# A seven-product MLP: the up stage makes two block sums of its activations and none of w_down, the down stage makes the others

## The chip, the core and the metric

The kernel runs on one core of a Trainium2 chip. The metric is the device time of one execution in microseconds. The core has five engines with queues of their own: TensorE (PE, with PEld for its weight loads), VectorE (DVE), ScalarE (ACT), GpSimd (POOL) and SyncE (SP, which here only issues transfers). ACT and POOL issue transfers too. A transfer of one block is 128x512 float32, 256 KB.

## The reference, cut to what matters

One decoder layer on 2048 tokens of width 1024: a token mixer, then an MLP with 4096 hidden units. Only the MLP is touched by the change:

```python
x = x + _rmsnorm(mix, norm_mix_post[i])
h = _rmsnorm(x, norm_mlp_pre[i])
f = jnp.square(jax.nn.relu(jnp.einsum("btd,df->btf", h, w_up[i])))
f = jnp.einsum("btf,fd->btd", f, w_down[i])
x = x + _rmsnorm(f, norm_mlp_post[i])
```

## The kernel before, in words

**Precision.** Every float32 operand of a large matmul is split into a high and a low part (`split`, L493 to L497: ACT copies the high part, L495, and DVE subtracts it, L496), and a product is three matmuls, high by high, high by low, low by high.

**Seven products for eight.** Both MLP matmuls are done on 2x2 blocks with the Strassen-Winograd scheme, which needs seven block products, numbered 0 to 6 and always walked in `ORDER` 0, 1, 5, 6, 4, 2, 3. The left operand of product 0 to 3 is a11, a12, s4, a22, of product 4, 5, 6 it is s1, s2, s3, where s1 = a21+a22, s2 = s1-a11, s3 = a11-a21, s4 = a12-s2 (`left`, L500). The right operands are b11, b21, b22, t4, t1, t2, t3 with t1 = b12-b11, t2 = b22-t1, t3 = b22-b12, t4 = b21-t2 (`right_sums`, L517).

**Mixer.** The mixer fills the first half of the time. It leaves the normed hidden states in DRAM (`h2_d`). `hidden_sums(g, k)` (L525) loads four blocks of them, scales them on ACT, makes t1 to t4 and stores seven blocks in `hs_d`. For g = 0 POOL makes these sums, for g = 1 DVE does. The pieces of work left over from the last mixer block stand in a list `pend` and are taken one by one inside the up stage by `drain(1)`, the four `hidden_sums(1, k)` as the last of them (steps 10 to 13 of g = 0).

**Up stage.** There are two token halves g, and for each of them 16 steps p, which are 32 steps. `hidden_blocks(g)` (L537) loads and splits the 28 right operands of a half, and they stay in SBUF for its 16 steps. A step is 7 products of 4 x 3 matmuls, 84 matmuls of 128x512. For it `up_weights` (L674) makes the four sums s1 to s4 of the next piece of w_up on DVE (L506, L507, L509, L512) into tiles of the tag `us`, which has 4 buffers, and splits seven operands (7 times L495 on ACT, 7 times L496 on DVE) into `wh` and `wl`, with 9 buffers each: little more than one step's. Seven additions (L708, DVE) take the products out of PSUM. ACT applies relu and square (L712, L713) and POOL makes the four sums of the activations (`summed`, L721: operands 4, 5, 6, 2 of the down stage). ACT stores the three plain blocks and POOL its four sums, so that all seven left operands of the down stage stand in DRAM (`f_d`).

**w_down in the up stage.** In 16 of the 32 steps (the table `due`, L842) four blocks of w_down are also loaded (`down_sums_load`, L677) and, behind the step, their t1 to t4 are made on DVE (`down_sums`, L686, by L519 to L522). These go to the same four `us` buffers, and from there by SP to DRAM (`dn_d`, L690).

**Down stage.** For each product in `ORDER` all 16 pieces p are accumulated in eight PSUM banks, one for each of eight sites (g, t). A step p is 8 sites x 3 matmuls, 24 matmuls (L822 to L824). `down_operands` (L748) loads one block of w (from w_down or `dn_d`) and one of f for each g, three transfers a step, and splits them. The f operands go round rings of eight steps (`ROUND`), w has 9 buffers, raw tiles of w have 6 (`raw`), raw tiles of f have 6 (`xt`). When a product is complete, `close` (L788) adds its eight banks to the accumulators. Products 2 and 3 end output rows: `half` squares and scales a half row (tile `us` for the squares), and `finish` (L769) loads the residual x1 in two tiles of the tag `uc` (10 buffers, L775), applies L776 on DVE and stores the result, one half by SP and one by ACT (L777). For the last product, 3, the last six steps are kept back and done site by site (`LATE`).

**What sets the order.** The program is written in the order above, and a scheduler (the tile framework) sorts each engine's queue by times that it estimates. The queue is then fixed, and each engine works through it in order and waits where an operand or a buffer is not there.

Of the kernel before, what the change touches and what calls it, by code (L numbers as in the profile page):

```python
# [44 lines left out]
def hybrid_layer(ctx: ExitStack, tc: tile.TileContext, x, xT, w_in, w_dt, w_out, w_up, w_down,  # L45
# [631 lines left out]
    def down_sums_load(p):  # L677
        raw = {}
        for j in range(2):
            for k in range(2):  # L680
                raw[j, k] = big("yl")
                SY.dma_start(raw[j, k].rearrange("p (a b) -> p a b", a=1),
                             w_down[2 * p + j][:, k:k + 1, :])
        return raw

    def down_sums(p, raw):  # L686
        blocks = right_sums(raw[0, 0], raw[0, 1], raw[1, 0], raw[1, 1], V)
        for i in ORDER:
            if i > 2:
                SY.dma_start(dn_d[p][i], blocks[i])  # L690

    turn = [0]

    def up(g, p, hb7, wb7):
# [24 lines left out]
        def summed(i, a, b, op):  # L719
            c = big("fs")  # L720
            G.tensor_tensor(c, a, b, op=op)  # L721
            save(i, c, G)
            return c

# [11 lines left out]
        t1 = summed(4, a21, a22, ALU.add)
        t2 = summed(5, t1, a11, ALU.subtract)
        summed(6, a11, a21, ALU.subtract)
        a12 = relu2(plus(u3, product(3)))
        save(1, a12, S)  # L740
        summed(2, a12, t2, ALU.subtract)
# [3 lines left out]
    ROUND = (HOMES[0], HOMES[2]), (HOMES[1], HOMES[3])  # L745
    step = [0]

    def down_operands(i, p):  # L748
# [8 lines left out]
        w = split(raw, ("wh", "wl"))
        f = []
        for g in range(NG):
            raw = big("xt")  # L760
            SY.dma_start(raw, f_d[g][p][i])
# [138 lines left out]
```

## Time and profile before

| | |
|---|---|
| runs shown | median 2867.87 us (2864.69 to 2868.1), 3 runs |
| the profiled execution | 2866.95 us |
| its span | 2865.2 us, 37725 instructions |
| mixer | to 1480 us |
| up stage | first matmul at 1480.3 us, last at 2226.9 us |
| down stage | 2226.8 us to 2855.0 us, then 10.2 us with no matmul |
| busy | PE 96%, PEld 78%, DVE 66%, ACT 47%, POOL 23% |
| moved by DMA | 456.81 MB, mean 159 GB/s |

In a row of the windows the columns are: the stretch in us, its length, then for PE, PEld, DVE, ACT and POOL the busy time and the count of instructions, then the granted clock of TensorE, the busy share of the 16 DMA engines, and GB/s. Matmuls overlap in the records, so that PE's busy time has to be read together with the count. In a row of the waits stand the waiting engine, tile and line, what it waited for, the sum in us, the number of times and the longest. In a row of the timeline stand start, duration, engine, line, operation, out<-in, count, and in square brackets the idle time before it and what ended it. In a group row the two numbers behind the bar are the busy time in us and the mean ns of one.

### The profile page before, as it was taken

The numbers are of one execution on the slowest core, as the hardware profiler recorded it, in microseconds if no ns is written. First come the engines' busy times: TensorE is split into PE (matmuls) and PEld (weight loads), VectorE is DVE, ScalarE is ACT, GpSimd is POOL, SyncE is SP. The second block draws the span as 40 slices with busy tenths as digits, with TensorE's granted clock in tenths as the row PEclk, the third lists the DMA queues.
The fourth block names the chain that finished last, engine by engine and source line by source line (L and its number), as shares of the span: only waits on it lengthen the run. The fifth ranks groups of instructions, "written<-read, shape, count | busy, mean of one in ns | idle before, by whom it ended". The sixth has DMA issues, their size and how long they took to land. (4 is left out here: it accounts for less than half of the span.)

```text
span 2865.2 us, 37725 instructions
## 1 busy us (share of the span) xinstructions
PE 2747.2 (96%) x12822; PEld 2247.6 (78%) x12822; DVE 1879.9 (66%) x3351; ACT 1351.6 (47%) x2361; POOL 646.8 (23%) x578
## 2 busy tenths in 40 slices
PE   8999999999999999999999989889989999999998
PEld 6888888888888887888877767767777788888877
DVE  6674867758676677766686666796677635434564
ACT  6545545564454645555554545454445533223331
POOL 1121412114121134211122433333333101000020
PEclk9999999999999999999999999999999999999999
DMA  7323344333343327443254658775654844444364
GB/s 276 131 85 121 100 129 143 119 107 107 119 144 125 108 93 255 150 147 113 97 167 147 225 175 279 262 241 200 210 192 153 292 140 135 144 139 140 122 199 146
DMA packets 254448, 456.81 MB, mean 159 GB/s; under 512 B 28080, under 2 KB 44848, under 8 KB 254256
## 3 DMA queue, kind: packets, MB, share of 16 engines
q1 hardware_dynamic: 198032, 359.50, 38.9%
q10 hardware_dynamic: 45984, 61.36, 6.1%
q0 software_dynamic: 10240, 33.56, 3.0%
q8 instruction: 100, 1.64, 0.2%
q14 instruction: 92, 0.75, 0.1%
HBM read 338.84 MB, written 115.47 MB: 159 GB/s over the span
## 5 line engine op out<-in xcount | busy, mean ns | idle before, releaser
L154 PE MATMUL mm<-hh,wh 128*128 128x512 f32 x1408 | 555.5, 395 | 5.4 <-DVE mix L444 3.2
L155 PE MATMUL mm<-hl,wh 128*128 128x512 f32 x1408 | 551.2, 391 | 0.8 <-DVE hl L144 0.8
L156 PE MATMUL mm<-hh,wl 128*128 128x512 f32 x1408 | 550.7, 391 | 0.0
L99 DVE TENSOR_TENSOR wl<-raw,wh 128x512 fp32r<-128x512 f32 x480 | 369.0, 779 | 236.7 <-ACT wh L98 228.0
L98 ACT CAST wh<-raw 128x512 fp32r<-128x512 f32 x480 | 293.0, 617 | 461.3 <-PE mm L155 292.8
L154 PEld LDWEIGHTS mm<-hh,wh 128*128 128x128 f32 x1408 | 265.8, 189 | 60.6 <-issue 4.5
L155 PEld LDWEIGHTS mm<-hl,wh 128*128 128x128 f32 x1408 | 265.8, 189 | 56.0 <-DVE hl L144 2.2
L156 PEld LDWEIGHTS mm<-hh,wl 128*128 128x128 f32 x1408 | 265.6, 189 | 55.7
L167 PE MATMUL ax<-wl,yh 128*128 128x512 f32 x512 | 200.5, 392 | 2.2 <-DVE wl L99 2.2
L166 PE MATMUL ax<-wh,yh 128*128 128x512 f32 x512 | 200.7, 393 | 0.0
L168 PE MATMUL ax<-wh,yl 128*128 128x512 f32 x512 | 200.4, 391 | 0.0
L496 DVE TENSOR_TENSOR wl<-raw,wh 128x512 fp32r<-128x512 f32 x163 | 118.9, 733 | 106.2 <-ACT wh L495 57.7
L822 PE MATMUL ax<-wh,hl 128*128 128x512 f32 x448 | 176.0, 394 | 8.1 <-DVE acc L785 6.5
L721 POOL TENSOR_TENSOR fs<-uc 128x512 f32<-128x512 f32 x64 | 87.0, 1359 | 416.7 <-ACT uc L713 250.4
L823 PE MATMUL ax<-wl,hl 128*128 128x512 f32 x448 | 175.7, 392 | 0.0
L496 DVE TENSOR_TENSOR wl<-us,wh 128x512 fp32r<-128x512 f32 x128 | 116.2, 916 | 84.9 <-POOL fs L721 38.8
L495 ACT CAST wh<-raw 128x512 fp32r<-128x512 f32 x163 | 100.2, 618 | 146.0 <-PE ax L824 68.2
L495 ACT CAST hl<-xt 128x512 fp32r<-128x512 f32 x120 | 74.3, 620 | 145.1 <-PE ax L823 102.9
L495 ACT CAST wh<-us 128x512 fp32r<-128x512 f32 x128 | 76.7, 617 | 129.0 <-POOL fs L721 36.8
L110 POOL TENSOR_TENSOR cst<-cst 128x1 f32<-128x1 f32 (+1 forms) x76 | 61.3, 807 | 337.4 <-DVE cst L109 332.9
L767 POOL TENSOR_TENSOR acc<-acc,gain 128x512 f32<-128x512 f32 x16 | 24.5, 1553 | 500.2 <-PE ax L824 338.4
L822 PE MATMUL mm<-wh,hh 128*128 128x512 f32 x336 | 131.3, 391 | 1.1 <-DVE uc L708 1.1
(455 smaller groups left out, 6171.3 us busy)
## 6 DMA issues: line engine op xcount, KB each, us to landing
raw<-w_in_dram SPq DMA_DIRECT2D x352, 256.0 KB, 2.8
xt<-f SPq DMA_DIRECT2D x224, 256.0 KB, 2.7
raw<-w_out_dram SPq DMA_DIRECT2D x128, 256.0 KB, 2.8
f<-fs POOLq DMA_DIRECT2D x128, 256.0 KB, 3.4
f<-uc ACTq DMA_DIRECT2D x96, 256.0 KB, 2.9
raw<-w_up_dram SPq DMA_DIRECT2D x68, 256.0 KB, 3.4
row<-cs SPq DMA_DIRECT2D x64, 256.0 KB, 4.0
yl<-w_down_dram SPq DMA_DIRECT2D x64, 256.0 KB, 4.4
```

The costliest lines, as they stand in the source:

```text
L98: S.copy(hi, raw)
L99: V.tensor_sub(lo, raw, hi.bitcast(F32))
L154: PE.matmul(pt, lhsT=wh[:, ks], rhs=ah[k], start=(k == 0), stop=False)
L155: PE.matmul(pt, lhsT=wh[:, ks], rhs=al[k], start=False, stop=False)
L156: PE.matmul(pt, lhsT=wl[:, ks], rhs=ah[k], start=False, stop=(k == KT - 1))
L166: PE.matmul(pts[t], lhsT=a, rhs=wh, start=(i == 0), stop=False)
L167: PE.matmul(pts[t], lhsT=a, rhs=wl, start=False, stop=False)
L168: PE.matmul(pts[t], lhsT=c, rhs=wh, start=False, stop=(i == n - 1))
L495: S.copy(hi, v)
L496: V.tensor_sub(lo, v, hi.bitcast(F32))
L822: PE.matmul(banks[k], lhsT=fh[:, ts], rhs=wh, start=(p == 0), stop=False)
L823: PE.matmul(banks[k], lhsT=fh[:, ts], rhs=wl, start=False, stop=False)
```

## The change

The up stage now stores six blocks a step: a11, a22, a21, a12 by ACT and s1, s2 by POOL (`summed` is gone, two POOL sums are left). `down_sums_load`, `down_sums`, `due` and `dn_d` are gone. In the down stage `down_operands` loads what an operand needs and makes the difference itself: `F_PARTS` names the blocks of f (two for products 2 and 6, subtracted on POOL into `fs`), `W_PARTS` those of w (two for products 4 and 6, and for product 3 with t2 as the second; three for product 5), subtracted on DVE into `us`. Product 5 stores its t2 by ACT for product 3. A step of products 0, 1, 5, 6, 4, 2, 3 then has 3, 3, 5 (and one store), 6, 4, 5, 4 loads, where each had 3.

The buffers move with it: `half` squares into `fs` instead of `us`; `finish` takes x1 into `us` (4 buffers) instead of `uc` (10); the rings of the low parts of f have seven places, no longer eight. `hidden_sums` is made by POOL for both halves.

```diff
-        blocks = right_sums(raw[0, 0], raw[0, 1], raw[1, 0], raw[1, 1], V if g else G)
+        blocks = right_sums(raw[0, 0], raw[0, 1], raw[1, 0], raw[1, 1], G)
...
-    ROUND = (HOMES[0], HOMES[2]), (HOMES[1], HOMES[3])
+    ROUND = (HOMES[0], HOMES[2][:7]), (HOMES[1], HOMES[3][:7])
...
+    F_PARTS = (("a11",), ("a12",), ("a12", "s2"), ("a22",), ("s1",), ("s2",), ("a11", "a21"))
+    W_PARTS = ((0, 0),), ((1, 0),), ((1, 1),), ((1, 0), None), ((0, 1), (0, 0)), \
+        ((0, 1), (0, 0), (1, 1)), ((1, 1), (0, 1))
...
+        ws = []
+        for at in W_PARTS[i]:
+            raw = big("raw")
+            if at is None:
+                SY.dma_start(raw, t2_d[p])
+            else:
+                j, k = at
+                SY.dma_start(raw.rearrange("p (a b) -> p a b", a=1),
+                             w_down[2 * p + j][:, k:k + 1, :])
+            ws.append(raw)
+        v = ws[0] if len(ws) == 1 else less(V, "us", ws[0], ws[1])
+        if len(ws) == 3:
+            v = less(V, "us", ws[2], v)
+            S.dma_start(t2_d[p], v)
+        w = split(v, ("wh", "wl"))
         f = []
         for g in range(NG):
-            raw = big("xt")
-            SY.dma_start(raw, f_d[g][p][i])
-            f.append(split(raw, [r[n % len(r)] for r in ROUND[g]]))
+            fs = []
+            for part in F_PARTS[i]:
+                fs.append(big("xt"))
+                SY.dma_start(fs[-1], f_d[g][p][part])
+            v = fs[0] if len(fs) == 1 else less(G, "fs", *fs)
+            f.append(split(v, [r[n % len(r)] for r in ROUND[g]]))
...
     def half(m, s2, tok, i, eng):
-        S.activation(big("us"), m, AF.Square, accum_out=s2[:, i:i + 1])
+        S.activation(big("fs"), m, AF.Square, accum_out=s2[:, i:i + 1])
...
         for i in range(2):
-            xt = big("uc")
+            xt = big("us")
             SY.dma_start(xt, x1_d[tok][:, i * 512:(i + 1) * 512])
...
-            if due[g][p]:
-                dn = ahead.pop(0)
-                draw = down_sums_load(dn)
             up(g, p, hb7, wb7)
             drain(1)
-            if due[g][p]:
-                down_sums(dn, draw)
```

**DVE in the second half of the up stage.** Before, the four sums of w_down (L519 to L522, reading `yl`) stand between the sums of w_up (L506 to L512), the splits (L496) and the additions out of PSUM (L708):

```order
L512 TENSOR_TENSOR us<-raw,us 128x512
L519 TENSOR_TENSOR us<-yl 128x512
L496 TENSOR_TENSOR wl<-us,wh 128x512 x2
L520 TENSOR_TENSOR us<-yl,us 128x512
L496 TENSOR_TENSOR wl<-raw,wh 128x512
L521 TENSOR_TENSOR us<-yl 128x512
L708 TENSOR_TENSOR uc<-uc,ax 128x512
L708 TENSOR_TENSOR uc<-uc,mm 128x512
L522 TENSOR_TENSOR us<-yl,us 128x512
L496 TENSOR_TENSOR wl<-yh,wh 128x512 x2
```

Now, at the same kind of place (the addition is L693 there):

```order
L512 TENSOR_TENSOR us<-raw,us 128x512
L496 TENSOR_TENSOR wl<-us,wh 128x512
L693 TENSOR_TENSOR uc<-uc,mm 128x512
L496 TENSOR_TENSOR wl<-us,wh 128x512
L693 TENSOR_TENSOR uc<-uc,ax 128x512
L506 TENSOR_TENSOR us<-yh 128x512
L693 TENSOR_TENSOR uc<-uc,mm 128x512
```

The four L519 to L522 rows are gone, and with them the other users of the four `us` buffers in this half.

**DVE at the passage from product 2 to product 3 in the down stage.** Before, the last splits ahead of product 2's first closing addition (L785) belong to product 3, those of its weights (`wl<-raw`) among them:

```order
L496 TENSOR_TENSOR wl<-raw,wh 128x512
L496 TENSOR_TENSOR m<-xt,hh 128x512
L496 TENSOR_TENSOR scm<-xt,hl 128x512
L496 TENSOR_TENSOR wl<-raw,wh 128x512
L496 TENSOR_TENSOR m<-xt,hh 128x512
L496 TENSOR_TENSOR xd<-xt,hl 128x512
L496 TENSOR_TENSOR wl<-raw,wh 128x512
L496 TENSOR_TENSOR m<-xt,hh 128x512
L496 TENSOR_TENSOR xdh<-xt,hl 128x512
L785 TENSOR_TENSOR acc<-acc,mm 128x512 x3
```

Now only splits of product 3's f blocks stand there. Its first weight difference (L734, `us<-raw`) and weight split (`wl<-us`) come behind all but one of the 16 L776 of `finish`, these rows being the end of them:

```order
L776 SCALAR_TENSOR_TENSOR us<-acc,cst,us 128x512
L109 TENSOR_SCALAR cst<-cst 128x1
L776 SCALAR_TENSOR_TENSOR us<-acc,cst,us 128x512 x5
L734 TENSOR_TENSOR us<-raw 128x512
L776 SCALAR_TENSOR_TENSOR us<-acc,cst,us 128x512
L496 TENSOR_TENSOR wl<-us,wh 128x512
L734 TENSOR_TENSOR us<-raw 128x512 x2
L496 TENSOR_TENSOR wl<-us,wh 128x512 x2
```

So the weights of product 3 moved from ahead of the closing of product 2 to behind its `finish`, since x1 and these differences share the four `us` buffers.

**SP at the same passage.** Now the loads of x1 (L775, `us<-x`) alternate with the stores of finished rows (L777), each load waiting for a `us` buffer:

```order
L777 DMA out_dram<-us 128x512
L775 DMA us<-x_2_79 128x512
L777 DMA out_dram<-us 128x512
L775 DMA us<-x_2_79 128x512
L775 DMA us<-x_3_80 128x512
L777 DMA out_dram<-us 128x512
L775 DMA us<-x_3_80 128x512
L775 DMA us<-x_8_85 128x512
```

Before, the ten tiles of tokens 0 to 3 and 8 were loaded ahead of the first of these stores; now the four of tokens 0 and 1.

More of the change, by code (lines that the diff above doesn't have):

```diff
@@ L475, in hybrid_layer @@
     ORDER = (0, 1, 5, 6, 4, 2, 3)
-    f_d = [[[dram.tile([P, TB], F32, name=f"f{g}_{p}_{i}") for i in B7]
+    f_d = [[{i: dram.tile([P, TB], F32, name=f"f{g}_{p}_{i}")
+             for i in ("a11", "a12", "a21", "a22", "s1", "s2")}
             for p in range(NP)] for g in range(NG)]
-    dn_d = [[dram.tile([P, 512], F32, name=f"dn{p}_{i}") if i > 2 else None for i in B7]
-            for p in range(NP)]
+    t2_d = [dram.tile([P, 512], F32, name=f"t2_{p}") for p in range(NP)]
     hs_d = [[[dram.tile([P, TB], F32, name=f"hs{g}_{i}_{k}") for k in range(4)]
@@ L675, in up_weights @@
         return left(raw[0, 0], raw[0, 1], raw[1, 0], raw[1, 1], V)
[L677 to L690, printed above, removed]
     turn = [0]
@@ L717, in save @@
             q.dma_start(f_d[g][p][i], c)
[L719 to L723, printed above, removed]
         s1 = big("uc")
@@ L727, in up @@
         a11 = relu2(plus(s1, product(1)))
-        save(0, a11, S)
+        save("a11", a11, S)
         u2 = plus(s1, product(5))
@@ L733, in up, with less @@
         a22 = relu2(plus(u3, p5))
-        save(3, a22, S)
+        save("a22", a22, S)
         a21 = relu2(plus(u4, product(2)))
[L736 to L741, printed above, removed]
+        save("a21", a21, S)
+        t1, t2 = big("fs"), big("fs")
+        G.tensor_tensor(t1, a21, a22, op=ALU.add)
+        save("s1", t1, G)
+        G.tensor_tensor(t2, t1, a11, op=ALU.subtract)
+        save("s2", t2, G)
+        save("a12", relu2(plus(u3, product(3))), S)
     LATE = 6
-    ROUND = (HOMES[0], HOMES[2]), (HOMES[1], HOMES[3])
+    ROUND = (HOMES[0], HOMES[2][:7]), (HOMES[1], HOMES[3][:7])
     step = [0]
+    F_PARTS = (("a11",), ("a12",), ("a12", "s2"), ("a22",), ("s1",), ("s2",), ("a11", "a21"))
+    W_PARTS = ((0, 0),), ((1, 0),), ((1, 1),), ((1, 0), None), ((0, 1), (0, 0)), \
+        ((0, 1), (0, 0), (1, 1)), ((1, 1), (0, 1))
+    def less(eng, tag, a, b):
+        c = big(tag)
+        eng.tensor_tensor(c, a, b, op=ALU.subtract)
+        return c
     def down_operands(i, p):
@@ L839, in down_stage @@
                 close(i, k, banks[k])
-    ahead = list(range(NP))
-    due = [[p in at for p in range(NP)] for at in
-           ((3, 5, 7, 9, 11, 13, 15), (3, 4, 6, 7, 8, 10, 11, 12, 14))]
     raw = up_load(0, 0)
```

7 lines of the change are left out of this document (removed).

## The prediction

> **What bounds the kernel now.** I read the page first, then the windows cut at the steps of the up stage, then PE's waits, then the timelines at two places. PE is busy for 96% of the span, so the question is where it is not, or at which clock.
>
> ```profile
> PE 2747.2 (96%) x12822; PEld 2247.6 (78%) x12822; DVE 1879.9 (66%) x3351; ACT 1351.6 (47%) x2361; POOL 646.8 (23%) x578
> ...
> 1480.27:1554.10 73.83, 66.18 (x273) 53.30 (x272) 46.37 (x65) 31.69 (x54) 17.47 (x18) 0.93 0.51 168
> 1554.10:1853.30 299.20, 266.55 (x1125) 212.85 (x1125) 205.25 (x299) 146.99 (x263) 107.34 (x111) 0.96 0.69 233
> 1853.30:1927.90 74.60, 61.18 (x253) 48.52 (x252) 71.89 (x94) 45.22 (x82) 24.98 (x24) 0.91 0.70 240
> 1927.90:2226.90 299.00, 278.72 (x1178) 223.87 (x1177) 210.44 (x285) 133.28 (x227) 106.91 (x112) 0.97 0.56 192
> 1927.90:1946.97 19.07, 19.07 (x86) 15.79 (x85) 13.41 (x17) 8.59 (x15) 7.78 (x8) 1.00 0.50 167
> 2007.50:2035.10 27.60, 22.96 (x85) 17.15 (x84) 17.09 (x27) 9.81 (x17) 7.68 (x8) 0.88 0.53 184
> 2330.00:2762.00 432.00, 432.00 (x1907) 357.48 (x1906) 190.58 (x285) 142.93 (x266) 15.50 (x12) 1.00 0.45 139
> ```
>
> The last row is PE undisturbed: 432.00 / 1907 = 0.2265 us a matmul, 5.44 us a down step of 24, 19.0 us an up step of 84. The row of 1927.90 is such an up step; that of 2007.50, the same work, took 27.6 us, at a granted clock of 0.88. Lost time of a stretch is its length less 0.2265 us a matmul: steps 0 and 1 of the first half 73.8 - 61.8 = 12.0; its steps 2 to 14 299.2 - 254.8 = 44.4; step 15 and steps 0 and 1 of the second half 74.6 - 57.3 = 17.3; the rest 299.0 - 266.8 = 32.2. That is 105.9 us in the up stage, while 2330 to 2762 of the down stage loses nothing. What PE waits for in the up stage:
>
> ```profile
> PE mm L703 <- DVE wl L496: 32.4, 14, 5.0
> PE mm L701 <- ACT wh L495: 18.7, 9, 6.0
> PE ax L703 <- DVE wl L496: 10.3, 9, 2.1
> ```
>
> So it waits for the split weights. DVE is not busy all the time there, but it is held up. Two rows of POOL and one of DVE show by what:
>
> ```profile
> 2017.63 1.30 POOL L721 TENSOR_TENSOR fs<-fs,uc 128x512 f32<-128x512 f32 x1
> 2018.88 1.28 POOL L721 TENSOR_TENSOR fs<-uc 128x512 f32<-128x512 f32 x1
> ...
> 2020.20 0.69 DVE L512 TENSOR_TENSOR us<-raw,us 128x512 f32<-128x512 f32 x1 [2.72 <-POOL fs L721]
> ...
> 2028.98 0.69 DVE L521 TENSOR_TENSOR us<-yl 128x512 f32<-128x512 f32 x1 [1.81 <-DMA f<-fs]
> ```
>
> DVE's L512, with two SBUF inputs, begins 0.04 us after POOL's second sum ends (2020.16). Such DVE operations and POOL's sums take turns. The last row is a stall inside a sum of w_down.
>
> ```profile
> 2009.88 0.69 DVE L708 TENSOR_TENSOR uc<-uc,mm 128x512 f32<-128x512 f32 x1 [1.98 <-DMA f<-fs]
> ...
> L721 POOL TENSOR_TENSOR fs<-uc 128x512 f32<-128x512 f32 x64 | 87.0, 1359 | 416.7 <-ACT uc L713 250.4
> L496 DVE TENSOR_TENSOR wl<-us,wh 128x512 fp32r<-128x512 f32 x128 | 116.2, 916 | 84.9 <-POOL fs L721 38.8
> ...
> L496 DVE TENSOR_TENSOR wl<-raw,wh 128x512 fp32r<-128x512 f32 x109 | 78.1, 717 | 89.1 <-ACT wh L495 50.0 <-PE ax L823 32.7 <-DMA uc<-x 5.3
> ...
> L495 ACT CAST wh<-us 128x512 fp32r<-128x512 f32 x128 | 76.7, 617 | 129.0 <-POOL fs L721 36.8
> ...
> L776 DVE SCALAR_TENSOR_TENSOR uc<-acc,cst,uc 128x512 f32<-128x512 f32 x32 | 25.7, 844 | 8.1 <-POOL cst L110 8.1
> ```
>
> The split itself agrees: 916 ns in the up stage (first L496 row), 717 in the down stage (second), where POOL is nearly idle.
>
> **The up stage, part by part.** I price a step as if DVE's operations with two SBUF inputs and POOL's sums never overlap. Before: 11 of the former (4 sums, 7 splits) at 0.69 = 7.6, 4 POOL sums at 1.36 = 5.4, 7 additions out of PSUM at 0.69 = 4.8, together 17.8 us, under PE's 19.0. A step that also makes sums of w_down has 4 x 0.69 = 2.8 more: 20.6, over it, with the stores' waits on top. After: 7.6 + 2.7 + 4.8 = 15.1 us, so that 3.9 us a step are spare. The Trainium skill, "SBUF — State Buffer", section "Who interferes with whom", has this as a lock on one port pair: a two-input VectorE instruction and a GpSimd one that reads SBUF block each other for the whole instruction. The three rows agree; by it the sum stays as it is below, and were the two engines independent, the steps that I charge for POOL's work would lose nothing and the gain of 70 would be 80.
>
> What stays lost: steps 0 and 1, which begin with `hidden_blocks`, 12.0. The passage between the halves splits 28 blocks, 28 x 0.69 = 19.3 us of DVE in one step; it had four sums of w_down as well (2.8, and a stall like the 1.81), so 17.3 falls to about 13. Steps 10 to 13 make `hidden_sums` on POOL now, four more sums of 1.36: 15.1 + 5.4 = 20.5, 1.5 us over PE's 19.0 in each, 6 us; made by DVE they would need 15.1 + 2.8 = 17.9 and lose nothing. The four steps that end rows of the mixer carry two POOL and two DVE operations more, by the nearest rows 2 x 1.36 + 2 x 0.84 = 4.4: 19.5, with their small operations 1 us over in each, 4 us. Together 12.0 + 13 + 10 + 1 = 36, where 105.9 were lost: **gain 70 us**. From below: only the DVE time of the 64 sums, 64 x 0.69 = 44. From above: all but steps 0 and 1, 94. I take the working between them, because steps without sums in the second half already run at 19.07. Removed transfers (64 loads, 64 stores on SP, 32 stores of f) cost nothing by themselves; ACT's extra store of a21 lies in 8.6 to 9.8 us of busy ACT out of 19.
>
> **The down stage, products 5, 6, 4, 2.** They gain loads, DVE and POOL work, and operands are far ahead: SP waits there for PE, that is, for a ring place to come free.
>
> ```profile
> SPq L761 <- PE ax L824: 257.0, 117, 12.0
> 2226.00:2244.00 18.00, 12.75 (x39) 8.73 (x38) 18.00 (x27) 14.06 (x27) 6.34 (x6) 0.72 0.97 340
> ```
>
> Products 5 and 6 move six blocks a step, 1.573 MB in 5.44 us, 289 GB/s; the window above moved 340 through the same buffers. Product 6 on the turn-taking pair: one difference and three splits 4 x 0.69 = 2.8, two POOL differences 2.7, 5.5 us against 5.44. Seven ring places are 38 us of lead, which absorbs that and a passing shortage. I take **0**, up to 15 lost if the lead runs out.
>
> **The passage from product 2 to product 3.** This is the cost. Before:
>
> ```profile
> 2758.52 0.39 PE L824 MATMUL ax<-wh,xdl 128*128 128x512 f32 x1
> 2758.74 0.39 PE L822 MATMUL mm<-wh,hh 128*128 128x512 f32 x1
> ...
> 2766.00 0.39 PE L824 MATMUL mm<-wh,row 128*128 128x512 f32 x1
> 2772.91 0.79 PE L822 MATMUL ax<-wh,hl 128*128 128x512 f32 x1 [6.52 <-DVE acc L785]
> ...
> 2777.69 0.40 PE L824 MATMUL mm<-wh,row 128*128 128x512 f32 x1
> ...
> 2754.73 1.88 DVE L785 TENSOR_TENSOR acc<-acc,mm 128x512 f32<-128x512 f32 x3
> ...
> 2767.13 2.41 DVE L776 SCALAR_TENSOR_TENSOR uc<-acc,cst,uc 128x512 f32<-128x512 f32 x2 [0.45 <-POOL cst L110]
> ...
> 2760.70 3.48 DVE L776 SCALAR_TENSOR_TENSOR uc<-acc,cst,uc 128x512 f32<-128x512 f32 x2 [0.46 <-POOL cst L110]
> 2768.91 1.00 ACTq L777 DMA_DIRECT2D out_dram<-uc  x2
> ...
> 2787.99 1.41 DVE L776 SCALAR_TENSOR_TENSOR uc<-acc,cst,uc 128x512 f32<-128x512 f32 x2 [0.44 <-POOL cst L110]
> ...
> xt<-f SPq DMA_DIRECT2D x224, 256.0 KB, 2.7
> ...
> uc<-x SPq DMA_DIRECT2D x32, 256.0 KB, 5.2
> out_dram<-uc SPq DMA_DIRECT2D x16, 256.0 KB, 2.1
> out_dram<-uc ACTq DMA_DIRECT2D x16, 256.0 KB, 3.8
> ```
>
> PE went on with product 3 at 2758.74, stopped at 2766.00 for a bank and restarted at 2772.91, the next 11 matmuls taking 4.8 us where 2.5 are due: 6.7 us of hole and 2 of clock, 8.7. After, PE needs product 3's first weights, and these stand on DVE behind the L776 of `finish`. If x1 is always there, the 16 L776 end at 2789.4 as before; with difference 0.69, copy 0.62 and split 0.69 PE starts at 2791.4. But x1 has four buffers. The first two tokens' L776 end by 2769.5, and three more rounds follow of L776 0.84, store 3.0 (the mean of 2.1 and 3.8) and load, 3.5 (an estimate: the 2.7 of a load of f and 0.8 of SP's queue) to 5.2: 7.3 to 9.0 us each. The last round ends at 2791.5 to 2796.6; I take 2794 and a restart at 2796. PE has been idle since 2758.7: 37.3 and 2 for the clock, 39.3, less the 8.7 of before: **loss 31 us**. From below 2791.4, 26; from above rounds of 12 us (before, ACT issued the first stores only at 2768.91, 4.7 us behind the end of the L776 that began at 2760.70), 2805.5 and 2807.5, 42.
>
> Behind that, a step of product 3 needs 0.69 + 3 x 0.69 = 2.8 us of DVE in 5.44 and has its f splits ready: nothing more. In the tail the eight `finish` share the four buffers again. A site closes every 4.4 us (below, the first two after the first), so a tile has 8.8 us from one token to the next but one, against a store and a load of 3.0 + 3.5 to 5.2 and L776: about 1 us lost, 0 to 6.
>
> ```profile
> 2826.44 0.69 DVE L785 TENSOR_TENSOR acc<-acc,mm 128x512 f32<-128x512 f32 x1 [19.05 <-PE mm L824]
> 2830.86 0.68 DVE L785 TENSOR_TENSOR acc<-acc,mm 128x512 f32<-128x512 f32 x1
> ...
> 2226.90:2240.00 13.10, 7.85 (x21) 4.79 (x20) 13.10 (x21) 11.66 (x22) 3.13 (x3) 0.67 0.94 320
> ```
>
> The start of the down stage (last row: 13.1 us with 21 matmuls, so 8.3 lost) has the same splits in the same order: 0, plus or minus 4.
>
> **The sum.** -70 + 0 + 31 + 1 = -38 us. Against the profiled execution, 2866.95 us (span 2865.2 and 1.75 around it), that is 2829; the median of the runs shown, 2867.87, is 0.9 higher: **2830 us**.
>
> **Rivals.**
> A. My forecast: 0.64. Its own range: a gain of 80 with a loss of 26, to a gain of 58 with a loss of 40 and 5 beside it: 2814 to 2855.
> B. The passage costs nothing more, since SP and ACT get x1 through in time and PE's hole stays near that of before: -70 + 1, 2799 us. For it: only four L776 wait for a load if landings take under 3 us. Against: the order itself puts product 3's weights behind `finish`, whatever the loads do. 0.05.
> C. The up stage stays short of DVE or ACT: steps with leftovers from the mixer and `hidden_sums` on POOL still lose, so only the 44 us come back, and the passage costs its 42: 2867 and no change, or 2856 with 31. For it: the four `us` buffers are still shared with `hidden_sums`, whose stores ACT issues in order behind POOL. 0.19, a quarter of it near no change.
> D. Slower: the transfers of products 5 and 6 don't keep up. At 192 GB/s, the rate of the second half of the up stage, six blocks take 8.2 us a step, 2.75 over PE's, 88 us in 32 steps; less 38 of lead, 50 lost; product 2 with five blocks 6.8 us, 22 more: -70 + 31 + 1 + 72 = +34, 2902 us. It decides from a loss of 38, that is 76 us of shortage in those 32 steps, 7.8 us a step or 202 GB/s. For it: four xt tiles a step go through six buffers, so that a tile may take 8.2 us from issue to issue, of which 5.2 can be the landing and 1.4 POOL. Against: 340 GB/s in the window above. 0.07.
> Half of what is left over, 0.05, I give to each side.
> The Trainium skill, "DMA: Bandwidth & Descriptors", section "Specifications", gives about 358 GB/s for a core's share of HBM, by which 289 fits and D would not come; no trace here shows a limit of that kind.
>
> About 0.2% (5.7 us) is what a measurement of this kernel can tell from no change. Faster by more: 0.86; within: 0.05; slower: 0.09. The range of 2805 to 2860 takes in A, most of C's milder half, and leaves out B's end and D.
>
> **What would show it.** Right: the windows of the up stage's second half at 19.0 to 19.2 us a step with granted clock 1.00; PE's waits for L496 and L495 there mostly gone; a single PE hole of 30 to 45 us between products 2 and 3, ended by DVE's split of `wl<-us`; products 5 and 6 with no idle PE. Wrong: holes in products 5 or 6 with DMA near its full share (D); up steps still at 20 us and more with DVE waiting for POOL or for `us` (C); a hole of under 20 us at the passage (B).

## The result, and the profile after

The changed kernel takes 2790.06 us, median of 4 runs (2788.24 to 2791.79), beside 2867.98 us for the kernel before on the same chip (2864.69 to 2868.7): ratio 0.973, 95% interval 0.9714 to 0.9747. The gain is 78 us where 38 were forecast, and the time lies 15 us under the range. The profiled span is 2787.5 us, 77.7 less. The page's first part, and the groups that stand for L496 with `us` and for one of POOL's two sums a step:

```profile
PE 2711.5 (97%) x12822; PEld 2235.0 (80%) x12822; DVE 1883.7 (68%) x3351; ACT 1351.6 (48%) x2361; POOL 639.9 (23%) x530
...
L496 DVE TENSOR_TENSOR wl<-us,wh 128x512 fp32r<-128x512 f32 x192 | 148.8, 778 | 114.6 <-ACT wh L495 65.8 <-PE ax L823 14.9 <-PE ax L824 6.9
...
L717 POOL TENSOR_TENSOR fs<-uc 128x512 f32<-128x512 f32 x32 | 42.6, 1332 | 398.2 <-ACT uc L698 208.6 <-DVE wl L496 85.7 <-PE mm L688 46.3
```

DVE, ACT and POOL are as busy as before. What changed is when. The windows at the same stages, then products 5 and 6, then the passage from product 2 to product 3:

```profile
1478.50:1546.50 68.00, 62.64 (x273) 51.07 (x272) 44.85 (x68) 31.01 (x54) 10.95 (x10) 0.97 0.54 179
1546.50:1801.50 255.00, 253.40 (x1125) 209.18 (x1125) 181.93 (x262) 146.87 (x268) 84.73 (x79) 0.99 0.61 206
1801.50:1863.00 61.50, 58.93 (x253) 46.84 (x253) 56.83 (x84) 41.75 (x76) 11.72 (x12) 1.00 0.70 238
1863.00:2129.70 266.70, 266.70 (x1178) 220.83 (x1177) 184.71 (x265) 143.28 (x244) 52.31 (x56) 1.00 0.42 146
2129.70:2142.90 13.20, 13.20 (x60) 10.94 (x59) 9.68 (x14) 6.80 (x13) 3.96 (x4) 1.00 1.01 356
2303.70:2390.70 87.00, 87.00 (x385) 72.04 (x384) 64.48 (x79) 30.30 (x56) 37.73 (x25) 1.00 0.85 293
2390.70:2477.70 87.00, 87.00 (x385) 72.06 (x384) 54.14 (x73) 27.34 (x48) 20.16 (x13) 1.00 0.68 226
2651.90:2686.10 34.20, 0.15 (x2) 0.07 (x1) 25.78 (x43) 8.03 (x23) 17.04 (x15) 0.57 0.67 213
```

By the prediction's measure (length less 0.2265 us a matmul) the up stage now loses 6.2, 0.2, 4.2 and -0.1 us in the four stretches, 10.5 where it lost 105.9: 95.4 us came from there. The start of the down stage, 13.2 us with 60 matmuls, loses nothing (9.6 before over the whole product 0). Products 5 and 6 have no idle PE. The passage costs a hole of 34 us. Together -95.4 - 9.5 + 27.7 (the passage, 37.0 lost where 9.3 were) + 1.3 (the tail) - 1.8 (the mixer) = -77.7 us. PE's waits from 1470 us on:

```profile
PE mm L822 <- ACT wh L495: 34.0, 1, 34.0
PE mm L686 <- ACT wh L495: 4.9, 1, 4.9
PE mm L687 <- DVE xdt L496: 1.9, 1, 1.9
PE ax L688 <- DVE wl L496: 1.4, 1, 1.4
```

The 61 us of waits for split weights in the up stage (the three rows shown for the kernel before) are down to 6. The one long wait is the passage; in its timeline stand PE's last matmul of product 2 and its first of product 3, and what DVE did between:

```profile
2651.60 0.39 PE L824 MATMUL ax<-wh,scm 128*128 128x512 f32 x1
2686.03 1.22 PE L822 MATMUL mm<-wh,hh 128*128 128x512 f32 x2 [34.05 <-ACT wh L495]
...
2647.27 2.05 DVE L785 TENSOR_TENSOR acc<-acc,mm 128x512 f32<-128x512 f32 x3 [10.87 <-PE mm L824]
...
2681.84 1.41 DVE L776 SCALAR_TENSOR_TENSOR us<-acc,cst,us 128x512 f32<-128x512 f32 x2 [3.43 <-DMA us<-x]
2683.98 0.75 DVE L776 SCALAR_TENSOR_TENSOR us<-acc,cst,us 128x512 f32<-128x512 f32 x1 [0.73 <-DMA us<-x]
2684.65 0.68 DVE L734 TENSOR_TENSOR us<-raw 128x512 f32<-128x512 f32 x1
```

Product 3's difference (L734) stands behind all but one of the L776, as forecast; the restart came 38.8 us behind the first L785, where 41.3 were forecast.

### The profile page after: what moved, and what is told of

Its sections match the earlier page's. It is cut to its first block, busy times and chain, and to the rows that moved or that the text cites. A ratio compares the mean times of both kernels' runs of the same rounds, so it can differ in the third digit from the quotient of the medians.

```text
span 2787.5 us, 37716 instructions
## 1 busy us (share of the span) xinstructions
PE 2711.5 (97%) x12822; PEld 2235.0 (80%) x12822; DVE 1883.7 (68%) x3351; ACT 1351.6 (48%) x2361; POOL 639.9 (23%) x530
## 4 chain that ended last, share of the span: by engine, by line
PE 90%; DVE 4%; DMA 3%; issue 1%; POOL 1%; ACT 1%; ACTq 0%; SPq 0%; DVEq 0%; POOLq 0%
PE mm L155 11%; PE mm L154 11%; PE mm L156 11%; PE ax L824 4%; PE ax L822 4%; PE ax L823 4%; PE ax L166 4%; PE ax L168 4%; PE ax L167 4%; PE ax L688 3%; PE ax L686 3%; PE ax L687 3%; PE mm L687 3%; PE mm L688 3%; PE mm L686 3%; PE mm L823 3%
## 5 line engine op out<-in xcount | busy, mean ns | idle before, releaser
L99 DVE TENSOR_TENSOR wl<-raw,wh 128x512 fp32r<-128x512 f32 x480 | 368.5, 778 | 241.7 <-ACT wh L98 230.5
L98 ACT CAST wh<-raw 128x512 fp32r<-128x512 f32 x480 | 293.0, 617 | 464.1 <-PE mm L155 294.3
L496 DVE TENSOR_TENSOR wl<-us,wh 128x512 fp32r<-128x512 f32 x192 | 148.8, 778 | 114.6 <-ACT wh L495 65.8
L495 ACT CAST wh<-us 128x512 fp32r<-128x512 f32 x192 | 114.7, 616 | 95.5 <-DVE us L509 26.6
L496 DVE TENSOR_TENSOR wl<-raw,wh 128x512 fp32r<-128x512 f32 x99 | 79.1, 803 | 107.9 <-ACT wh L495 56.8
L734 POOL TENSOR_TENSOR fs<-xt 128x512 f32<-128x512 f32 x64 | 94.9, 1490 | 197.9 <-DMA xt<-f_s 99.4
L717 POOL TENSOR_TENSOR fs<-uc 128x512 f32<-128x512 f32 x32 | 42.6, 1332 | 398.2 <-ACT uc L698 208.6
L823 PE MATMUL mm<-wl,hh 128*128 128x512 f32 x336 | 131.6, 392 | 0.3 <-DVE wl L496 0.3
L697 ACT ACTIVATE uc<-uc 128x512 f32<-128x512 f32 x128 | 80.7, 631 | 101.2 <-DVE uc L693 89.6
```

What stands on the lines that cost most here:

```text
L98: S.copy(hi, raw)
L99: V.tensor_sub(lo, raw, hi.bitcast(F32))
L496: V.tensor_sub(lo, v, hi.bitcast(F32))
L823: PE.matmul(banks[k], lhsT=fh[:, ts], rhs=wl, start=False, stop=False)
```

## The experiments

Three theories of the unexpected gain in the up stage are tried: **turns** (DVE's operations with two SBUF inputs and POOL's sums exclude each other, the prediction's price), **held buffers** (the four `us` buffers wait for SP's stores), **transfers** (the loads and stores of the w_down sums were not free). For the passage, **order** (product 3's split behind `finish`) stands against **four buffers** for x1.

The table gives all runs. "Lost" is length less 0.2265 us a matmul between the first matmuls of the steps, from the profiled run; steps 2 to 14 hold small mixer matmuls that are shorter, so that -3.4 there is nothing lost. (The windows above also count matmuls that reach across an edge, hence 6.2 there and 6.4 here.) The ratio is to the kernel before as measured beside that run; its median there was 2862.58 to 2867.98 us, so that the times alone don't tell apart runs that differ by less than 5 us. "Lead" is how long before PE's first matmul with an operand DVE had ended its split, the mean of the seven operands of the step.

| run | time us (ratio to before, 95%) | lost: steps 0-1 | 2-14 | 15-17 | 18-31 | product 0 | products 2, 3 | lead at step 24, 31 |
|---|---|---|---|---|---|---|---|---|
| before | 2867.98 | 12.3 | 44.6 | 17.5 | 32.5 | 9.6 | 9.3 | 1.0, 7.5 |
| after | 2790.06 (0.9714-0.9747) | 6.4 | 0.4 | 4.4 | 0.2 | 0.1 | 37.0 | 16.0, 20.1 |
| e1 | 2770.18 (0.9669-0.9698) | 7.1 | -3.4 | 5.7 | 0.2 | 0.1 | 20.4 | 16.0, 20.1 |
| e2 | 2850.22 (0.9947-0.9976) | 9.6 | 61.0 | 16.7 | 2.8 | 12.1 | 9.1 | 7.6, 3.3 |
| e3 | 2801.01 (0.9779-0.9808) | 10.3 | 28.9 | 11.9 | 0.2 | 1.9 | 8.3 | 7.7, 12.8 |
| e4 | 2784.87 (0.9723-0.9754) | 8.5 | 14.9 | 10.3 | 0.2 | 5.5 | 10.0 | 16.8, 12.0 |
| e5 | 2785.22 (0.9698-0.9733) | 8.5 | -3.4 | 1.9 | 0.2 | 0.1 | 37.8 | 16.0, 20.1 |
| e6 | 2807.18 (0.9766-0.9809) | 11.9 | 5.6 | 9.6 | 0.2 | 0.1 | 38.0 | 14.7, 18.3 |
| e7 | 2873.65 (1.0016-1.0037) | 10.0 | 39.1 | 13.4 | 19.3 | 8.3 | 37.5 | 1.8, 5.8 |
| e8 | 2780.89 (0.9682-0.9718) | 9.8 | -1.1 | 6.4 | 0.2 | 0.1 | 27.5 | 16.0, 20.1 |
| e9 | 2767.7 (0.9641-0.967) | 8.2 | -3.4 | 3.2 | 0.2 | 0.1 | 19.7 | 16.0, 20.1 |
| e10 | 2758.95 (0.961-0.9639) | 8.1 | -3.4 | 4.6 | 0.2 | 0.1 | 8.3 | 16.0, 20.1 |
| e11 | 2761.29 (0.9619-0.9652) | 7.2 | -1.7 | 6.4 | 0.2 | 0.1 | 6.0 | 16.0, 20.1 |
| e12 | 2801.11 (0.9753-0.9782) | 8.6 | 36.2 | 4.9 | 0.2 | 0.1 | 8.8 | 10.8, 18.7 |
| e13 | 2827.48 (0.9852-0.9885) | 7.1 | 38.6 | 2.6 | 0.2 | 0.1 | 36.9 | 15.8, 20.1 |
| e14 | 2800.14 (0.9755-0.9786) | 7.8 | -0.8 | 14.5 | 0.2 | 0.1 | 38.6 | 15.2, 19.4 |
| e15 | 2752.51 (0.9593-0.9621) | 8.5 | -3.4 | 3.8 | 0.2 | 0.1 | 6.1 | 16.0, 20.1 |
| e16 | 2830.77 (0.9865-0.9894) | 12.6 | 31.5 | 10.8 | 0.2 | 0.1 | 36.2 | 16.2, 18.4 |
| e17 | 2812.0 (0.9799-0.9829) | 10.8 | 30.9 | 7.1 | 12.2 | 1.2 | 9.1 | 1.2, 13.4 |
| e18 | 2864.13 (0.9984-1.0005) | 14.1 | 58.8 | 12.2 | 21.1 | 10.5 | 9.1 | 1.3, 4.0 |

### The two parts alone: e3 and e4

e3 is the kernel before with the activation part (two POOL sums, the rest in the down stage; rings of seven, squares in `fs`):

> The kernel before with the activation part of the change alone: two sums on POOL in the up stage, differences of f on POOL in the down stage (with the rings of seven and the squares of half in fs, without which it does not fit into SBUF); the sums of w_down stay in the up stage, in the us buffers. T1: a step with sums needs 7.6 + 2.8 + 2.7 + 4.8 = 17.9 us, under PE's 19.0, so some 60 us come back: 2800 to 2815 us. T2: the us buffers are held as before, at most 25 us come back: 2843 to 2868 us.

e4 is the changed kernel with the four activation sums back on POOL, `hidden_sums` of g = 1 on DVE and x1 in `uc`:

> The w_down part of the change alone: no sums of w_down in the up stage, differences of w on DVE in the down stage; the four activation sums stay on POOL in the up stage, hidden_sums of the second half stays on DVE, and x1 stays in the uc buffers. T1: 17.8 us a step, under 19.0, the ordinary steps lose nothing but those with hidden_sums (20.6) and mixer leftovers (over 21) lose 15 or so: 2805 to 2820 us. T2: all the ordinary steps are free, those with hidden_sums lose some us as their sums sit in the us buffers: 2785 to 2800 us. If POOL's four sums are what lengthens steps 0 and 1, the passage between the halves and the start of the down stage, these lose 12, 13 and 8 us as before; if not, they are shorter by themselves.

Either part alone takes away the whole loss of steps 18 to 31, so that loss needed both. By the table, up stage and product 0 together lost 116.5 us before; e3 takes away 63 of it, e4 77, the whole change 105. The two parts are 140 together, 35 too many, and 32 of these are what both regain in steps 18 to 31. Elsewhere the gains nearly add: in steps 2 to 14 they are 15.7 and 29.7, and the whole change gains 44.2. The hole of the passage is in neither part (8.3 and 10.0 us lost in products 2 and 3).

### What the turns cost: e7, e6, e14

More POOL sums in each up step, four in e7 and, with `range(2)`, two in e6:

```diff
         save("s2", t2, G)
+        for _ in range(4):
+            G.tensor_tensor(big("fs"), a21, a22, op=ALU.add)
```

> The same with four more unread POOL sums a step, six in all. Turn-taking in full: 7.6 + 6 x 1.36 + 4.8 = 20.6 us a step against PE's 19.04; 1.5 us in each of 14 undisturbed steps of the second half, 21 us, 1.5 us in those of the first, 20, and the disturbed steps as with two more sums: 2835 to 2855 us, with up steps of 20.5 us in a row. If POOL's work displaces DVE only where an operation with two SBUF inputs happens to meet a sum (DVE's additions out of PSUM can lie beside them): second half 19.04, 2795 to 2812 us.

Windows of e7 over steps 18 to 23, 25 to 29, 30 and 31, then POOL and DVE in step 26:

```profile
1914.30:2028.50 114.20, 114.20 (x505) 94.57 (x504) 78.75 (x103) 52.39 (x93) 51.03 (x45) 1.00 0.39 134
2048.70:2151.50 102.80, 98.02 (x421) 78.03 (x420) 74.11 (x94) 45.24 (x81) 46.01 (x39) 1.00 0.34 121
...
2151.50:2176.50 25.00, 22.03 (x85) 17.70 (x84) 11.97 (x19) 10.68 (x18) 13.05 (x12) 0.86 0.28 103
2176.50:2199.90 23.40, 19.23 (x85) 15.61 (x84) 15.21 (x21) 15.67 (x29) 11.40 (x11) 0.99 0.45 147
```

```profile
2069.03 6.07 POOL L722 TENSOR_TENSOR fs<-uc 128x512 f32<-128x512 f32 x4
...
2068.76 2.13 DVE L496 TENSOR_TENSOR wl<-raw,wh 128x512 fp32r<-128x512 f32 x1 [3.67 <-DMA f_s<-fs]
2070.82 1.77 DVE L507 TENSOR_TENSOR us<-us,raw 128x512 f32<-128x512 f32 x1
2072.52 0.67 DVE L693 TENSOR_TENSOR uc<-uc,mm 128x512 f32<-128x512 f32 x1
2075.13 0.69 DVE L509 TENSOR_TENSOR us<-raw 128x512 f32<-128x512 f32 x1 [1.94 <-POOL fs L722]
```

Five steps took 102.8 us, 20.56 each, where the turns give 20.6: the price of a step was right there. But six steps at the same price before them took 19.03 each (114.2 / 6). They lived on a lead, which fell from 8.6 us at step 19 to 1.8 at step 24; from there PE paid. The last two steps took 25.0 and 23.4 us, more than the turns give, and no run shows why. Beside POOL's four sums a split and a sum of DVE with two SBUF inputs took 2.13 and 1.77 us, the addition out of PSUM its usual 0.67. The total is 19 to 39 us over the expected one, most of it in the first half, where the lead is short: it was 2.5 and 0.1 us at steps 11 and 12, which lost 8.1 and 11.1 us.

> The changed kernel with two more POOL sums in each up step, which nobody reads and nobody stores, so four POOL sums a step as before, without their stores and with no w_down sums. The run with four stored sums lost 34.9 us in the first half and passage where the changed kernel loses 11. If POOL's time is what cost that: second half 17.8 us of turns a step, 0 lost; first half and passage 10 to 20 more: 2800 to 2810 us. If the stores and the buffers that they hold cost it: 2790 us within 4.

It cost 17.1 us, nearly all before step 18 (10.7 us more lost up to step 14, 5.2 in steps 15 to 17), with nothing stored: the work of the sums is a cost of its own. e4 and e9 differ in the whole activation part, with the stores of the two sums. e4 takes 17.2 us longer, but that equals e6's cost by chance: up to step 17 it loses 25.7 us more and in product 0 5.4, while e9 loses 9.7 more in products 2 and 3. So what goes with the sums, their stores perhaps, costs some too; no run has it apart.

e14 adds `right_sums(raw[0, 0], raw[0, 1], raw[1, 0], raw[1, 1], V)` on tiles of w_up in the 16 steps of `due`, with nothing stored or read:

> The changed kernel with four unread DVE sums in the same steps, made from tiles of w_up that are there anyway, with no loads and no stores. Turns on the mean of the steps: 17.9 us a step against 19.04, nothing lost in the second half, 0 to 5 in the first: 2790 to 2795 us. Each heavy step by itself, as the prediction priced it: 17.9 us are under PE's time too, but the steps with mixer leftovers and with hidden_sums on POOL go to 22 and 23, 20 to 30 us: 2810 to 2820. Transfers: 2790 within 3.

It cost 10.1 us, at one place. Windows of step 16 and of the second half:

```profile
1820.60:1854.10 33.50, 24.66 (x86) 18.88 (x85) 30.79 (x48) 22.70 (x42) 4.03 (x5) 0.80 0.78 249
1854.10:2139.00 284.90, 284.90 (x1259) 235.90 (x1258) 219.46 (x317) 149.90 (x254) 58.58 (x60) 1.00 0.42 146
```

Step 16, with the 28 splits, has 30.8 us of DVE in 33.5. Everywhere else the 2.8 us a step cost no time at once, but they used up lead: at step 16 it is 2.4 us, where the changed kernel has 8.9.

### What the transfers cost: e13, e16

e13 puts the loads and stores of the w_down sums back into the steps of the changed kernel, without the sums:

```diff
+            if due[g][p]:
+                dn = ahead.pop(0)
+                draw = down_sums_load(dn)
             up(g, p, hb7, wb7)
             drain(1)
+            if due[g][p]:
+                for n, jk in enumerate(draw):
+                    SY.dma_start(dn_d[dn][n], draw[jk])
```

> The changed kernel with the transfers of the sums of w_down put back into the steps that made them before (four loads, four stores on SP, 2.1 MB a step), and without the sums: the stores take the loaded tiles, nobody reads what they leave. Turns of DVE and POOL: nothing added, 2790 us within 3. Transfers: at the 350 to 368 GB/s that the steps with hidden_sums reached when they lost, 2.1 MB are 5.7 to 6.0 us a step; the steps 11 and 13 of the first half and the passage between the halves, which carry 285 to 304 GB/s without them, lose 10 to 25 us more; the second half, at 138 GB/s, loses nothing: 2800 to 2815 us.

It cost 37.4 us, all in steps 6 to 13. Windows of its steps 11 and 12:

```profile
1724.40:1760.30 35.90, 21.07 (x78) 16.57 (x79) 14.82 (x22) 15.27 (x26) 10.45 (x10) 0.79 0.98 340
1760.30:1785.00 24.70, 22.41 (x87) 17.77 (x86) 11.31 (x16) 8.11 (x14) 8.52 (x7) 0.88 0.97 348
```

No engine is full there, the transfers are. But the trace also shows that the scheduler had issued all 64 loads between 1482 and 1773 us, where the kernel before issued 35 in the first half. e16 ties each piece to its step by a DVE copy of one column of that step's a11 into each tile:

> The run with the transfers of the w_down sums alone, mended: there the scheduler issued all 16 pieces between 1482 and 1778 us, 33.5 MB more in the first half, where the kernel before moved 8 or 9 pieces. Here a DVE copy of one column of the step's a11 into each tile holds the stores, and with them the ring of the loads, to their steps. If transfers cost by the amount in the first half: half of 37 us or less, 2797 to 2809 us, nothing in the second half. If the 37 came only from all 16 pieces meeting hidden_sums: 2790 to 2796. If the stores in SP's order cost, whatever the rate: losses in the second half too, 2800 to 2820 with steps of over 19.1 us there.

It cost 40.7 us, none of it in steps 18 to 31. Windows of e16's first half and of its second:

```profile
1550.00:1810.00 260.00, 242.00 (x1034) 194.57 (x1033) 160.32 (x259) 135.56 (x245) 77.76 (x75) 0.97 0.67 225
1862.00:2172.00 310.00, 303.52 (x1322) 248.46 (x1321) 214.36 (x349) 166.00 (x286) 66.50 (x64) 0.99 0.62 212
```

The tie has a price of its own: DVE sat idle before the copies for 12.9 us in ten places. So the transfers, at the amount of the kernel before, cost between 28 and 41 us in the first half and nothing in the second, with the lead of 15 us there. Whether by their rate alone (e13: 340 to 348 GB/s) or by SP's order (e16's steps are at 0.45 to 0.88 of the DMA engines) stays open.

### Held buffers: e2 and e12, mended as e18 and e17

The sums of w_down get tiles of `acc` instead of `us`, in the kernel before (e2) and in e3 (e12):

```diff
-        blocks = right_sums(raw[0, 0], raw[0, 1], raw[1, 0], raw[1, 1], V)
+        blocks = right_sums(raw[0, 0], raw[0, 1], raw[1, 0], raw[1, 1], V, "acc")
```

> The kernel before with one edit: the four sums of w_down go to buffers of the tag acc, which nothing else uses in the up stage, no longer to the four us buffers. All DVE and POOL operations and all transfers stay. Theory T1 (engine time: DVE's two-input operations and POOL's sums take turns and do not fit in PE's 19.0 us): a step with sums still needs 20.6 us, so at least 16 x 1.6 = 25 us stay lost on top of the steps 0, the passage between the halves and the leftovers; 2830 to 2868 us. Theory T2 (buffers: the sums hold the us buffers until SP, which issues in order, has stored them, and the next step's sums of w_up wait): 60 to 75 of the 76 us lost in the ordinary up steps come back, 2793 to 2808 us.

> The kernel before with the activation part of the change alone (two POOL sums a step, 2801.0 us), and the sums of w_down in acc buffers. It lost 51 us in the first half and at the passage between the halves, although the turns add up to less than PE's time on the mean of its steps: 17.9 us in a step with sums of w_down. If what it lost there is the us buffers, held until SP's stores have been issued: 20 to 36 us come back, 2766 to 2782 us. If it is DVE's time for those sums: 2801 us within 6.

Both were misleading. With more buffers the scheduler pulled the pieces forward: 49 of 64 loads in the first half in e2, 63 in e12. e2's quiet second half had 15 of these loads, where the kernel before had 29. e17 and e18 tie each piece to its step, as e16 does; the column of a11 overwrites one column of b12, so that t1 to t4 are changed there.

> The kernel before with the activation part alone and the sums of w_down in acc, mended in the same way (there 15 of the 16 pieces were made in the first half): each piece's sums wait for its step's a11. Held us buffers: with us free the first half and the passage lose 15 to 35 us instead of 51, 2766 to 2785 us. DVE's and the transfers' time as it is: 2795 to 2803 us.

> The kernel before with only the home of the w_down sums changed to acc, mended in the same way (there 13 of the 16 pieces went to the first half, so that its quiet second half proves nothing). Turns with a lead: nine of the 14 undisturbed steps of the second half take 20.6 us of turns and five 17.8, 8 us over PE's time in sum, which a lead of up to 16 us hides: with us free the 32.5 us lost there fall to under 10, 2830 to 2845 us. If turns alone make the loss, without the buffers: 32 us remain, 2855 to 2870.

e18 takes as long as the kernel before, e17 11 us more than e3. DVE sat idle ahead of the tying copy for 4.6 us in e18 (4.3 of them in steps 18 to 31) and 13.1 in e17. Freeing the buffers in this way brings nothing on the whole. But the tie costs more than its own waits: e17 loses 12.2 us in steps 18 to 31, where e3, with the sums in `us` and no tie, loses 0.2. That e3 loses nothing there shows that held buffers alone don't make the loss. How much they add to the rest is shown only from below: 11 to 16 us of the 32.5 in steps 18 to 31 (e18 loses 21.1 there, 16.8 without the tie's waits).

### hidden_sums: e5

e5 is the changed kernel with `hidden_sums` of g = 1 back on DVE:

```diff
-        blocks = right_sums(raw[0, 0], raw[0, 1], raw[1, 0], raw[1, 1], G)
+        blocks = right_sums(raw[0, 0], raw[0, 1], raw[1, 0], raw[1, 1], V if g else G)
```

> The changed kernel with hidden_sums of the second group back on DVE, as before the change; all else as changed (2790.1 us). Turn-taking: four POOL sums of 1.36 leave steps 10 to 13 and four DVE sums of 0.69 come, 17.9 us a step instead of 20.5, so the 3.9 us that these steps still lose go: 2786 us. Rival, held buffers: DVE now waits for the four us buffers while ACT issues the stores of the hidden sums in order, as in the kernel with four POOL sums and no w_down sums, where these steps lost 9.1 us: 2795 us. Neither (in the run with x1 in uc, POOL's hidden sums cost 0): 2790 us within 1.5.

It gained 4.8 us, with overlapping intervals; in the profiles 3.8 of it are in steps 2 to 14, where the prediction had 6 for POOL and 0 for DVE. But with x1 in `uc` (e1) the same sums on POOL lost nothing there, so 3.8 us are the most that POOL costs, not its price in every order.

### The passage: e1, e8, e11

e1 puts x1 back, `xt = big("uc")` in `finish`:

> The changed kernel with one edit undone: finish takes x1 into the ten uc buffers again, no longer into the four us buffers. Theory (the four shared buffers put product 3's weights behind finish): the 34 us hole of PE between products 2 and 3 falls to the 7 or so of the kernel before, the rest stays, so 2790 - 28 = 2762 us, between 2758 and 2768. Rival (the hole is the closing of product 2 itself, which now waits for DVE and POOL longer whatever the buffers are): the hole stays over 25 us and the time between 2782 and 2790.

The hole of 34 us falls apart, as PE's waits in the timeline show:

```profile
2655.04 0.76 PE L822 MATMUL mm<-wh,hh 128*128 128x512 f32 x1 [5.28 <-DVE acc L785]
2659.20 0.50 PE L822 MATMUL ax<-wh,hh 128*128 128x512 f32 x1 [0.48 <-DVE cst L109]
2668.76 0.80 PE L822 MATMUL ax<-wh,hl 128*128 128x512 f32 x1 [6.28 <-DVE acc L785]
```

e8 adds POOL for product 3's difference: `less(G if i == 3 else V, "us", ws[0], ws[1])`.

> The changed kernel with x1 of finish back in uc and product 3's difference of w_down made by POOL. With x1 in uc alone 2770.2 us: between products 2 and 3 PE stood 5.67 us at 2649.4, where DVE's closing additions stood in its queue behind L734's waits for raw (1.65, 2.13 and 1.06 us idle), and 6.67 us at 2662.1. If those waits are the cause of the first hole: 2764 to 2767 us. If the closing additions wait for something else: 2770 within 2. If POOL, in order behind half's multiplications and finish, becomes late with the sums: 2775 to 2790 us.

It is worse than e1 by 10.7 us: the sums waited 3.8 to 4.6 us each for `raw<-t`, and the holes of 5.3 and 6.3 us grew to 11.4 and 10.3. The loads were late, not DVE.

e11 leaves x1 in `us` and takes product 3's difference away: product 5 makes the fourth sum too and stores it in the place of the second.

```diff
-    W_PARTS = ((0, 0),), ((1, 0),), ((1, 1),), ((1, 0), None), ((0, 1), (0, 0)), \
-        ((0, 1), (0, 0), (1, 1)), ((1, 1), (0, 1))
+    W_PARTS = ((0, 0),), ((1, 0),), ((1, 1),), (None,), ((0, 1), (0, 0)), \
+        ((0, 1), (0, 0), (1, 1), (1, 0)), ((1, 1), (0, 1))
...
-        if len(ws) == 3:
+        if len(ws) == 4:
             v = less(V, "us", ws[2], v)
-            S.dma_start(t2_d[p], v)
+            S.dma_start(t2_d[p], less(V, "us", ws[3], v))
```

> The changed kernel, x1 still in us, with the fourth sum made and stored in product 5 as in the run above. It parts the two halves of the passage's 37.0 us: x1 through four buffers alone, with nothing of product 3's weights in them. If the hole is the order (product 3's split behind finish in DVE's queue): 9 to 12 us lost, 2762 to 2768 us. If four buffers for x1 are the price by themselves, because finish holds banks and DVE until its loads have landed: 15 us lost and more, 2770 to 2780.

Products 2 and 3 lose 6.0 us where they lost 37.0, less than in the kernel before. The splits of product 3 stand ahead of the closing additions again, and PE's one longer wait is short:

```profile
2645.00 0.69 DVE L496 TENSOR_TENSOR wl<-raw,wh 128x512 fp32r<-128x512 f32 x1 [3.29 <-ACT wh L495]
...
2650.70 0.69 DVE L785 TENSOR_TENSOR acc<-acc,mm 128x512 f32<-128x512 f32 x1 [0.21 <-PE mm L824]
...
2660.97 0.50 PE L822 MATMUL ax<-wh,hh 128*128 128x512 f32 x1 [3.29 <-DVE acc L785]
```

So the passage is the order, and x1 in four buffers costs nothing by itself. Product 5 moves seven blocks a step here and still loses nothing.

### The best version: e9, e10, e15

e9 is e1 with e5, e10 is e9 with the fourth sum stored, e15 is e11 with e5.

> The changed kernel with both single edits that gained: x1 of finish in uc (2770.2 us) and hidden_sums of the second group on DVE (4.9 us less than the changed kernel). If the two act at different places their gains add: 2765 to 2767 us. If the steps with hidden_sums lose nothing once x1 is elsewhere (as in the run with x1 in uc alone) only the passage between the halves is left to gain, 5.6 to about 2 us lost: 2766 to 2768. Rival, no sum of gains: 2770.

> The kernel with both edits, and product 5 makes the fourth sum of w_down too (one more load, one more DVE difference a step) and stores it in the place of the second, so that product 3's weights are one load with no difference in front of the split. Theory, the shared us buffers and DVE's difference in front of product 3's split make the passage between products 2 and 3: it falls from 20.4 us lost to the 9 of the kernel before: 2754 to 2758 us. Rival, transfers: product 5 now moves seven blocks a step, 1.835 MB in 5.44 us, 337 GB/s; if it can't, each 10 GB/s short is 0.17 us a step, and at 290 GB/s 0.9 us a step, 14 us lost in product 5: 2768 to 2775.

> The kernel with the fourth sum stored and x1 in us (2761.3 us), with hidden_sums of the second group on DVE: 4.9 us less than that by the run that changed this alone, 2756 to 2758 us; with x1 in uc the same edits gave 2759.0, so if us is no worse a home for x1 than uc it is at or under that.

The edit of e5, which gained 4.8 us alone, gives 2.5 on top of e1 (e9, with overlapping runs) and 8.8 on top of e11 (e15); of these three only the last is clear of the 5 us. e15 is the fastest, 2752.51 us (2750.8 to 2755.4), ratio 0.9607, interval 0.9593 to 0.9621: 37.6 us under the changed kernel. Its up stage from step 2 to 14 and its second half:

```profile
1550.00:1801.00 251.00, 251.00 (x1125) 208.14 (x1124) 185.77 (x280) 146.49 (x266) 61.59 (x63) 1.00 0.61 208
1861.00:2126.70 265.70, 265.70 (x1173) 219.99 (x1173) 184.17 (x264) 143.31 (x243) 52.32 (x56) 1.00 0.42 146
```

## Why the prediction was wrong, point by point

**The up stage, -70 forecast, -95.4 measured: the step that failed.** Of the 36 us that it kept, 10.5 were left: steps 0 and 1 lost 6.2 us and not 12, the passage between the halves 4.2 and not 13, `hidden_sums` on POOL at most 3.8 and not 6, the mixer leftovers 0 and not 4. Two sentences are wrong, and the first of them made most of the 25.5 us by which this term is off.

The first is the reckoning step by step: every step over PE's 19.0 us was charged its excess. The price per step was right (20.56 measured, 20.6 worked out, e7). But steps are joined by a lead: split weights stand ready, and a heavy step draws on what light ones laid up. In the changed kernel DVE reached the rings' end (here step 24, whose first matmul is PE's row):

```profile
1960.09 0.69 DVE L496 TENSOR_TENSOR wl<-raw,wh 128x512 fp32r<-128x512 f32 x1 [0.87 <-POOL fs L717]
...
1966.43 0.69 DVE L496 TENSOR_TENSOR wl<-us,wh 128x512 fp32r<-128x512 f32 x1 [0.27 <-PE ax L687]
...
1977.27 0.39 PE L686 MATMUL mm<-hh,wh 128*128 128x512 f32 x1
```

The same split (the first of the two in the row) and matmul in the kernel before:

```profile
2051.89 1.29 DVE L496 TENSOR_TENSOR wl<-raw,wh 128x512 fp32r<-128x512 f32 x2
...
2054.17 0.39 PE L701 MATMUL mm<-hh,wh 128*128 128x512 f32 x1
```

It ended the split 16.5 us ahead, and three splits later it waits for PE to free a place; in the kernel before it was 1.6 us ahead, and the mean lead at this step was 1.0 us. The passage between the halves goes with the lead too: at step 16 it was 1.0 us before, and the step lost 14.4 us; in the changed kernel 8.9 and 4.3; in e14 2.4 and 14.5. It is not all there: e6 and e7 lose 9.5 and 13.4 us in this step at leads of 8.4 and 9.7. For steps 0 and 1 the lead explains nothing: at step 0 it is 6 us in both kernels, and why they lose less is not shown (e6's two POOL sums bring 5.5 us back, but runs with the up stage unchanged differ there by 3.4).

The second is "Removed transfers (64 loads, 64 stores on SP, 32 stores of f) cost nothing by themselves". Put back alone they cost 37.4 us (e13), and 40.7 with the tie's own waits of up to 12.9 (e16), in the first half, where mixer leftovers, `hidden_sums` and the loads of the next half move as well. It is the largest single part, beside 17.1 for POOL's two sums (e6) and 10.1 for DVE's sums (e14). So the sentence gave the 44 us of steps 2 to 14 too narrow a cause; that most of them go was forecast. Added one at a time the three come to 55 to 68 us of the 105 of up stage and product 0. The rest would arise where they meet; no run shows it, and none takes the transfers alone out of the kernel before.

**The second half, 32.2 us, all but 1 forecast to go: right.** The 14 steps take 19.04 us each. The cause is only half settled: the turns, 19.6 us a step on the mean of nine steps with sums (20.6) and five without (17.8), are 8 us over PE in 14 steps. Either part's removal takes the whole loss (e3, e4), and held buffers are at least 11 to 16 (e18). No run shows where what is left, 8 to 13 us at most, comes from.

**The start of the down stage, 0 plus or minus 4 forecast, -9.5 measured: wrong, for the same reason.** The splits are the same and their order nearly so, but DVE comes to them with a lead of 20.1 us and not 7.5. The runs fall into groups by it: a lead at step 31 of 18 us and more loses 0.1 (the changed kernel and twelve runs), 12 to 13.4 loses 1.2 to 5.5 (e3, e4, e17), 3.3 to 7.5 loses 8 and more (before, e2, e7, e18). The rate there is as high as before (356 GB/s, 321 before).

**Products 5, 6, 4, 2, forecast 0: right.** 87.0 us each. Rival D is out: even seven blocks a step in product 5 lost nothing (e10, e11).

**The passage, +31 forecast, +27.7 measured: right**, in place and cause (e11). One term was too large: the rounds of x1 through four buffers were to add 4.6 us to what the order alone gives (36.7 us from the first L785 to the restart), and the restart came 2.1 us behind that. The rounds delay it only because product 3's difference stands behind them (e11).

**The tail, +1 forecast, +1.3 measured: right.** Rivals B and C are out: the passage cost its hole, and the up stage kept less, not more.

## What to carry to other kernels

Price a stage by its sum over many steps and the lead that its buffers allow, not step by step: a small excess is free as long as light steps refill the lead, and what a lead has saved comes back at the next passage. Do not put removed transfers at nothing where the stretch that they leave has other loads to make. An experiment that frees buffers or drops a dependence also moves the work, so count in the trace where it went before reading its time.
